# Holding back the first store and the fifth load until four loads have landed, in a gate-and-dispatch kernel

## The chip, the cores and the metric

The kernel runs on one core of a Trainium2 chip. The metric is the device time in microseconds (us) of one execution. Every profile below is one profiled execution; its "span" goes from the first to the last instruction of the program and is about 2 us shorter than the device time.

## The reference

For each of 16 x 1024 = 16384 tokens, the router has 8 logits. The two largest probabilities are taken and scaled to add up to one; each token's row of 512 numbers is then written twice, once for each of the two, multiplied by its weight.

```python
probs = softmax(router_logits)                       # over 8 experts
topk_probs = the two largest of probs, smaller first
topk_probs = topk_probs / sum(topk_probs)
out = x[:, :, None, :].repeat(2, axis=2) * topk_probs[..., None]
```

The input x has 33.6 MB, the logits 0.5 MB, the output 67.1 MB, all float32.

## The kernel before

Tokens are laid over 128 partitions, M = 128 tokens to a partition. `top2_weights` (lines 14 to 43) is done once for all tokens: one load of the logits (line 74), a small tournament of maxima and minima on VectorE that ends with the difference of the two largest logits (line 39), and two sigmoids on ScalarE (lines 41 and 42), which give the two weights `WA`.

The rest is one loop (line 77) over 16 chunks of L = 8 tokens per partition. Each chunk does three things:

- line 80: a load of 2 MB (2048 KB), issued by SyncE, from x into a tile `xg`. The pool `xbufs` has four buffers, so the first four loads are issued at once and each later load waits until the multiply four chunks earlier has freed its buffer.
- line 82: one multiply on VectorE, 128 x 8192, which reads `xg` twice through a broadcast and writes the tile `og`. The pool `obufs` has three buffers, so from the fourth chunk on a multiply waits until an earlier store has landed.
- line 88: a store of 4 MB (4096 KB), issued by ScalarE, from `og` to the output.

The loads stand in SyncE's queue and the stores in ScalarE's, each in order: what stands behind a waiting issue waits as well. Both queues are served by the same 16 DMA engines; in the profile the loads are queue q1 and the stores queue q10. The semaphores, the buffer assignment and the order on each queue are made by a scheduler when the program is built. Chunks, loads, multiplies and stores are counted from 0 in numbers (load 3 is the fourth).

Of the kernel before, what the change touches and what calls it, by code (L numbers as in the profile page):

```python
# [1 line left out]

# [4 lines left out]

F32 = mybir.dt.float32
ALU = mybir.AluOpType
ACTF = mybir.ActivationFunctionType  # L10
P = 128


def top2_weights(nc, pool, logits, M, E):

    hi, lo, n = None, None, E
    while n > 1:  # L20
        n //= 2
        if hi is None:
            a, b = logits[:, :, 0:n], logits[:, :, n : 2 * n]
            nhi = pool.tile([P, M, n], F32, tag=f"hi{n}")
            nlo = pool.tile([P, M, n], F32, tag=f"lo{n}")
            nc.vector.tensor_tensor(nhi, a, b, op=ALU.max)  # L26
            nc.vector.tensor_tensor(nlo, a, b, op=ALU.min)  # L27
        else:
            a, b = hi[:, :, 0:n], hi[:, :, n : 2 * n]
            nhi = pool.tile([P, M, n], F32, tag=f"hi{n}")  # L30
            nlo = pool.tile([P, M, n], F32, tag=f"lo{n}")
            tmp = pool.tile([P, M, n], F32, tag=f"tmp{n}")
            nc.vector.tensor_tensor(tmp, lo[:, :, 0:n], lo[:, :, n : 2 * n], op=ALU.max)  # L33
            nc.vector.tensor_tensor(nlo, a, b, op=ALU.min)  # L34
            nc.vector.tensor_tensor(nlo, nlo, tmp, op=ALU.max)  # L35
            nc.vector.tensor_tensor(nhi, a, b, op=ALU.max)  # L36
        hi, lo = nhi, nlo
    dlt = pool.tile([P, M], F32, tag="dlt")
    nc.vector.tensor_tensor(dlt, hi[:, :, 0], lo[:, :, 0], op=ALU.subtract)  # L39
    WA = pool.tile([P, M, 2], F32, tag="WA")  # L40
    nc.scalar.activation(WA[:, :, 0], dlt, ACTF.Sigmoid, scale=-1.0)  # L41
    nc.scalar.activation(WA[:, :, 1], dlt, ACTF.Sigmoid, scale=1.0)  # L42
    return WA


@with_exitstack
def kernel(
    ctx: ExitStack,
    tc: tile.TileContext,
    x: bass.AP,  # L50
    router_logits: bass.AP,
    k: bass.AP,
    out: bass.AP,
):
    nc = tc.nc
    B, S, D = x.shape
    E = router_logits.shape[-1]
    N = B * S
    assert int(k) == 2 and E == 8 and N % P == 0
    M = N // P  # L60

    L = 8
    x_v = x.rearrange("b s d -> (b s) d").rearrange("(p m) d -> p m d", p=P)
    o_v = out.rearrange("b s k d -> (b s) k d").rearrange("(p m) k d -> p m k d", p=P)
    rl_v = router_logits.rearrange("b s e -> (b s) e").rearrange(
        "(p m) e -> p m e", p=P
    )

    wpool = ctx.enter_context(tc.tile_pool(name="wpool", bufs=1))
    xbufs = ctx.enter_context(tc.tile_pool(name="xbufs", bufs=4))  # L70
    obufs = ctx.enter_context(tc.tile_pool(name="obufs", bufs=3))

    logits = wpool.tile([P, M, E], F32)
    nc.sync.dma_start(logits, rl_v)  # L74
    WA = top2_weights(nc, wpool, logits, M, E)

    for c in range(M // L):
        rows = slice(c * L, (c + 1) * L)
        xg = xbufs.tile([P, L, D], F32, tag="xg")
        nc.sync.dma_start(xg, x_v[:, rows, :])  # L80
        og = obufs.tile([P, L, 2, D], F32, tag="og")
        nc.vector.tensor_tensor(  # L82
            og,
            xg.unsqueeze(2).to_broadcast([P, L, 2, D]),
            WA[:, rows, :].unsqueeze(3).to_broadcast([P, L, 2, D]),
            op=ALU.mult,
        )
        nc.scalar.dma_start(o_v[:, rows], og)


# [1 line left out]
_INS = ['x', 'router_logits', 'k']  # L92
_OUTS = [((16, 1024, 2, 512), 'float32')]

_NUMBERS = {'k': 2}


# [26 lines left out]
```

## Time and profile before

| what | value |
|---|---|
| device time, median of 3 (lowest to highest) | 246.81 us (245.37 to 248.87) |
| span of the profiled execution | 244.8 us |
| VectorE busy, of which the 16 multiplies | 142.6 us, 138.9 us |
| one multiply (line 82) | 8.69 us |
| one load, 2048 KB: median from issue to landing | 42.3 us |
| one store, 4096 KB: median from issue to landing | 35.6 us |
| moved in all, mean rate over the span | 101.19 MB, 413 GB/s |

The page's digit rows cut the span into 40 slices of 6.1 us and give the busy share of each in tenths. "DMA" is the mean busy share of the 16 DMA engines, and "GB/s" is what they moved. The time from issue to landing holds the time in which a transfer stood behind others in its queue. The chain of waits goes back from the last instruction to what released it, and so on; "DMA out_dram<-og" is a store, "DMA xg<-in_x_dram" a load, "DVE og L82" a multiply. In tables of stretches each row names the stretch, its length, each engine's busy time with the number of instructions in it, the TensorE clock (unused here), the DMA engines' busy share and the rate.

### The profile page before, as it was taken

How to read it: one execution, taken by the hardware profiler on the slowest of the kernel's cores; microseconds unless marked ns; L12 is line 12 of the kernel's file. 1: busy time of each engine (PE TensorE's matmuls, PEld its weight loads, DVE VectorE, ACT ScalarE, POOL GpSimd, SP SyncE). 2: the span in 40 equal slices, each digit the busy share in tenths (PEclk: the TensorE clock that was granted, in tenths of full speed). 3: DMA queues.
4: the chain of work that ended last, by engine and by line, in shares of the span. 5: the costliest groups of instructions: out<-in, count | busy, mean ns of one | idle time of the engine just before them, and what ended most of it. 6: DMA issues, size and time to landing. Idle time of an engine off the chain costs nothing.

```text
span 244.8 us, 149 instructions
## 1 busy us (share of the span) xinstructions
DVE 142.6 (58%) x27; ACT 1.8 (1%) x3; POOL 0.2 (0%) x4
## 2 busy tenths in 40 slices
DVE  3799978549093580936729185391763908585000
ACT  2000000000000000000000000000000000000000
POOL 0000000000000000000000000000000000000000
DMA  7999999899999999999999999999999999999981
GB/s 300 428 428 332 439 428 471 385 436 452 428 439 412 428 458 420 396 428 431 442 439 420 426 447 407 452 404 399 466 423 415 426 418 434 428 428 428 434 369 86
DMA packets 4752, 101.19 MB, mean 413 GB/s; under 512 B 528, under 2 KB 528, under 8 KB 656
## 3 DMA queue, kind: packets, MB, share of 16 engines
q10 hardware_dynamic: 2304, 67.11, 63.9%
q1 hardware_dynamic: 2448, 34.08, 33.4%
HBM read 34.08 MB, written 67.11 MB: 413 GB/s over the span
## 4 chain that ended last, share of the span: by engine, by line
DMA 69%; DVE 21%; issue 0%; SPq 0%; DVEq 0%
DMA out_dram<-og 66%; DVE og L82 21%; DMA xg<-in_x_dram 3%; SPq L74 0%; DVEq L82 0%
## 5 line engine op out<-in xcount | busy, mean ns | idle before, releaser
L82 DVE TENSOR_TENSOR og<-xg,WA 128x8192 f32<-128x8192 f32 x16 | 138.9, 8691 | 77.2 <-DMA out_dram<-og 75.9
L26 DVE TENSOR_TENSOR nhi<-logits 128x512 f32<-128x512 f32 x1 | 0.7, 693 | 3.9 <-DMA logits<-in_router_logits_dram 3.9
L41 ACT ACT_TABLE_LOAD x1 | 1.3, 1283 | 0.7 <-PEq L105 0.7
L34 DVE TENSOR_TENSOR nlo<-nhi 128x256 f32<-128x256 f32 (+1 forms) x2 | 0.7, 353 | 0.0
L36 DVE TENSOR_TENSOR nhi<-nhi 128x256 f32<-128x256 f32 (+1 forms) x2 | 0.7, 353 | 0.0
L33 DVE TENSOR_TENSOR tmp<-nlo 128x256 f32<-128x256 f32 (+1 forms) x2 | 0.7, 352 | 0.0
L35 DVE TENSOR_TENSOR nlo<-nlo,tmp 128x256 f32<-128x256 f32 (+1 forms) x2 | 0.7, 352 | 0.0
L27 DVE TENSOR_TENSOR nlo<-logits 128x512 f32<-128x512 f32 x1 | 0.7, 683 | 0.0
L41 ACT ACTIVATE WA<-dlt 128x128 f32<-128x128 f32 x1 | 0.3, 315 | 5.7 <-DVE dlt L39 5.7
L39 DVE TENSOR_TENSOR dlt<-nhi,nlo 128x128 f32<-128x128 f32 x1 | 0.3, 291 | 0.0
L42 ACT ACTIVATE WA<-dlt 128x128 f32<-128x128 f32 x1 | 0.3, 299 | 0.0
L105 POOL MEMSET const-bfloat16-1.0<- 128x1 bf16 x1 | 0.1, 103 | 0.0
L105 POOL MEMSET const-uint8-127<- 128x1 uint8 x1 | 0.1, 102 | 0.0
L105 POOL MEMSET const-float32-0.0<- 128x1 f32 x1 | 0.1, 100 | 0.2 <-issue 0.2
L105 POOL MEMSET const-float32-1.0<- 128x1 f32 x1 | 0.1, 99 | 0.0
## 6 DMA issues: line engine op xcount, KB each, us to landing
out_dram<-og ACTq DMA_DIRECT2D x16, 4096.0 KB, 35.6
xg<-in_x_dram SPq DMA_DIRECT2D x16, 2048.0 KB, 42.3
logits<-in_router_logits_dram SPq DMA_DIRECT2D x1, 512.0 KB, 3.1
```

Source lines behind the costliest of these rows:

```text
L26: nc.vector.tensor_tensor(nhi, a, b, op=ALU.max)
L27: nc.vector.tensor_tensor(nlo, a, b, op=ALU.min)
L33: nc.vector.tensor_tensor(tmp, lo[:, :, 0:n], lo[:, :, n : 2 * n], op=ALU.max)
L34: nc.vector.tensor_tensor(nlo, a, b, op=ALU.min)
L35: nc.vector.tensor_tensor(nlo, nlo, tmp, op=ALU.max)
L36: nc.vector.tensor_tensor(nhi, a, b, op=ALU.max)
L39: nc.vector.tensor_tensor(dlt, hi[:, :, 0], lo[:, :, 0], op=ALU.subtract)
L41: nc.scalar.activation(WA[:, :, 0], dlt, ACTF.Sigmoid, scale=-1.0)
L42: nc.scalar.activation(WA[:, :, 1], dlt, ACTF.Sigmoid, scale=1.0)
L82: nc.vector.tensor_tensor(og, xg.unsqueeze(2).to_broadcast([P, L, 2, D]), WA[:, rows, :].unsqueeze(3).to_broadcast([P, L, 2, D]), op=ALU.mult,
L105: nc = _bacc.Bacc("TRN2", target_bir_lowering=False, num_devices=1)
```

## The change

Two dependencies are added by hand, both on the landing of load 3 (the fourth, `AHEAD - 1`): load 4 is not issued before load 3 has landed, and neither is the store of chunk 0. The purpose is to have the first four input buffers filled before any output traffic takes part of the DMA engines.

```diff
+    AHEAD = 4
+    sync = mybir.DependencyInfo(
+        mybir.DependencyClass.Sync, mybir.DependencyReason.DATA
+    )
+    gate = None
     for c in range(M // L):
         rows = slice(c * L, (c + 1) * L)
         xg = xbufs.tile([P, L, D], F32, tag="xg")
-        nc.sync.dma_start(xg, x_v[:, rows, :])
+        load = nc.sync.dma_start(xg, x_v[:, rows, :])
+        if c == AHEAD - 1:
+            gate = load.ins.name
         og = obufs.tile([P, L, 2, D], F32, tag="og")
...
+        if c == AHEAD:
+            tc.add_manual_dep(load.ins, gate, sync, reason="join")
-        nc.scalar.dma_start(o_v[:, rows], og)
+        store = nc.scalar.dma_start(o_v[:, rows], og)
+        if c == 0:
+            first = store
+        if c == AHEAD - 1:
+            tc.add_manual_dep(first.ins, gate, sync, reason="join")
```

The instructions are the same in kind and number. In the program that the scheduler builds from this, the first stores on ScalarE's queue stand in another order than in the source (the tile numbers are those of the program: og_91 is chunk 0, og_96 chunk 1, og_101 chunk 2):

```
L97 out<-og_96    waits for VectorE (the multiply of chunk 1)
L97 out<-og_91    waits for the landing of load 3
L97 out<-og_101   waits for VectorE (the multiply of chunk 2)
```

The loads and the multiplies stand in the order of the source. The multiply of chunk 3 writes the buffer that chunk 1 used, and the multiply of chunk 4 the buffer of chunk 0.

## The prediction

> **What bounds the kernel now.** I began with the page's slices and queue totals, since a kernel that only multiplies and copies is likely bound by data movement.
>
> ```profile
> span 244.8 us, 149 instructions
> DVE 142.6 (58%) x27; ACT 1.8 (1%) x3; POOL 0.2 (0%) x4
> DMA  7999999899999999999999999999999999999981
> GB/s 300 428 428 332 439 428 471 385 436 452 428 439 412 428 458 420 396 428 431 442 439 420 426 447 407 452 404 399 466 423 415 426 418 434 428 428 428 434 369 86
> DMA packets 4752, 101.19 MB, mean 413 GB/s; under 512 B 528, under 2 KB 528, under 8 KB 656
> q10 hardware_dynamic: 2304, 67.11, 63.9%
> q1 hardware_dynamic: 2448, 34.08, 33.4%
> ```
>
> The reader is to see that the DMA digit is 8 or 9 from the second slice to the third-last: the two queues' packets fill 63.9% + 33.4% = 97.3% of the time of 16 engines. VectorE is busy only 58%. Next the waits (the second line is SyncE's queue):
>
> ```profile
> DVE og L82 <- DMA out_dram<-og: 75.9, 13, 7.1
> SPq L80 <- DVE og L82: 152.5, 12, 15.1
> ```
>
> Thirteen multiplies wait for a store to land, so that an output buffer comes free; twelve loads wait for a multiply to free an input buffer; after the first one no multiply waits for a load. This ring is driven by how fast stores land. The chain of waits in order of time gives the beginning of it:
>
> ```profile
> 1.15 7.74 DMA xg<-in_x_dram
> ...
> 8.99 8.70 DVE og L82
> 17.70 0.02 issue
> 17.72 19.83 DMA out_dram<-og
> 37.55 0.03 DVEq L82
> 37.58 0.04 issue
> 37.63 8.70 DVE og L82
> ```
>
> The first load lands at 8.9, the first multiply ends at 17.7, the first store leaves then and takes 19.8 us. Last, the stretches of time (length, VectorE, ScalarE and GpSimd busy, clock, DMA share, GB/s):
>
> ```profile
> 10.00:18.00 8.00, 8.00 (x2) 0.00 (x0) 0.00 (x0) 1.00 1.01 432
> 18.00:24.00 6.00, 6.00 (x1) 0.00 (x0) 0.00 (x0) 1.00 1.01 336
> 24.00:60.00 36.00, 27.24 (x4) 0.00 (x0) 0.00 (x0) 1.00 1.00 432
> 60.00:200.00 140.00, 79.26 (x10) 0.00 (x0) 0.00 (x0) 1.00 1.01 429
> 208.00:236.00 28.00, 12.40 (x2) 0.00 (x0) 0.00 (x0) 1.00 1.00 432
> 236.00:244.80 8.80, 0.00 (x0) 0.00 (x0) 0.00 (x0) 1.00 0.33 142
> ```
>
> This is the table on which the forecast rests. Loads alone (10 to 18) move at 432 GB/s, loads and stores mixed (24 to 60) at 432, stores alone (208 to 236) at 432. Keeping loads and stores apart therefore buys no rate. The span can be rebuilt: the first packet moves at 1.7 us, 101.19 MB / 432 GB/s = 234.2 us, and the losses are 0.3 us at the start (1.2 to 9 us ran at 387), 6 x (1 - 336/432) = 1.3 us when the first store starts, 140 x (1 - 429/432) = 1.0 us in the middle, and 8.8 x (1 - 0.33) = 5.9 us at the end, where a few of the 16 engines still work after the others are done. The sum is 1.7 + 234.2 + 0.3 + 1.3 + 1.0 + 5.9 = 244.4, against a span of 244.8. Bytes and these losses are all there is.
>
> **What the Trainium skill says.** "DMA: Bandwidth & Descriptors", section "Issuing engines are not separate DMA queues": transfers issued by different engines run on the same 16 DMA engines and interleave. The same page, "Queues, rings and completion order", has each engine take turns between its queues packet by packet. The trace agrees: stores (4.2 MB) and loads (2.1 MB) share 432 GB/s, and 6.29 MB / 432 = 14.6 us is the pace at which VectorE's later multiplies follow each other (14.5 to 15.8 us from the fourth to the fifteenth). The same page, "Anatomy of one DMA", gives about 2.0 us of fixed cost for a transfer, most of it the confirmation after the last byte. The logits load agrees: 3.1 us from issue to landing, of which 0.52 MB / 432 = 1.2 us is data, leaves 1.9 us.
>
> **The change part by part.** *The two dependencies in the program.* They add no instruction that moves data, so bytes, multiplies and buffers are as before. In the built program the scheduler has also put chunk 1's store ahead of chunk 0's on ScalarE's queue: the first store issued waits for the second multiply, and chunk 0's store, right behind it, for the fourth load. The fourth multiply takes chunk 1's output buffer, the fifth that of chunk 0, so buffers come free in the order of the stores.
>
> *The fifth load waits.* Loads 0 to 2 land at 8.9, 13.8 and 18.7 us (issues at 1.15, 1.6 and 2.1 plus 7.7, 12.2 and 16.6 to landing), so one load by itself takes 4.9 us. The fourth landed at 30.0 before (issued at 2.6, 27.4 to landing), since the first store and the fifth load joined it. With both held back it lands at 18.7 + 4.9 = 23.6. The fifth load, before issued at 17.7, is issued then. Queued behind it on SyncE is only the sixth load, which needs the second multiply's end at 26.3 anyway.
>
> *The hole in the DMA.* Up to 23.6 the engines have only the four loads, and the fifth is not handed over until the semaphore of the fourth has fired. So the engines run dry from the last byte of load 3 until the first byte of load 4: exactly the fixed part of one transfer, seen once. From below it is the time from issue to the first packet: the logits issue at 0.73 shows its first packet at 1.70, so 1.0 us. From above it is the 1.9 us of the logits plus the 0.3 us of the slow beginning, plus about 0.5 us for engines that finish early (in the landing records the engines of one early load lie 0.4 us apart): 2.7 us. I take 1.9, since the logits load contains both ends of it.
>
> *The first store waits.* Stores leave at 26.3 instead of 17.7, 8.6 us later. I price this at nothing, and the work that hides it is the loads: from about 24.7 load 4 has 4.9 us of bytes, and load 5 is issued at 26.3, so the engines have loads until store packets arrive. Stores moved back are loads moved forward. With the 19.8 us of the first store before, the first store lands near 26.3 + 19.8 = 46.1, and the fourth multiply starts there instead of at 37.6. Does either queue run dry after that? Load 7 can be issued when that multiply ends, near 54.9; loads 4, 5 and 6 are in the queue by 34.9, and at one load per 14.6 us they last to about 67. Three stores are in the queue by 34.9, and last to about 46.1 + 2 x 14.6 = 75; the next joins at 54.9. So both queues stay filled, by 12 us and more. At the end more stores run without loads beside them, at the same 432 GB/s, and with 9.7 us each (4.19 MB / 432) against 8.7 us for a multiply and three output buffers, VectorE keeps up.
>
> *The 1.3 us loss when the first store starts* I leave in place at its new time, because a load is again under way when the first store and another load are issued together. The stragglers' 5.9 us stay too: nothing in the change touches the engines' balance after 60 us.
>
> **Sum.** Span 244.8 + 1.9 = 246.7; the times are 2.0 us above the span (246.8 against 244.8), so 246.8 + 1.9 = 248.7 us, 0.8% slower, which 2% does not tell from no change.
>
> **The rivals.** *The hole is hidden or pays for itself.* The three times before spread from 245.4 to 248.9. If the loss of 1.3 us at the first store comes from the crowd of issues at 17.7 and goes away, the net is 1.9 - 1.3 = 0.6, so 247.4. For it: the later stores show no such loss. Against: a first store with loads under way is what the changed kernel has too. Chance 0.20.
>
> *Faster.* The engines that finish late could be put out of step by the first mixing, and a common restart at 23.6 could keep them together. With the 5.9 us gone: 248.7 - 5.9 = 242.8; with the 1.3 us gone too: 241.5, which alone is beyond 2% (below 241.9). For it: the fourth load, the first to be mixed, is the first whose landing stretches far beyond its 4.9 us. Against: from 24 to 60 the mixed rate is the full 432, so the lag is made later, where the change does not reach. Chance 0.10 in all, 0.03 beyond 2%.
>
> *Slower: the stores are the real path.* The chain of waits is 66% stores, and if it could not be caught up, the 8.6 us of late start would stand: 246.8 + 8.6 = 255.4. For it: every multiply from the fourth on waits for a store. Against: a store takes 35.6 us in the median only because it shares the engines with loads; with loads ahead, later stores go faster (stores alone at 432, from 208 on). Chance 0.06.
>
> **How the numbers follow.** Forecast 248.7 with 0.64; its cost bounds of 1.0 to 2.7 us give 247.8 to 249.5, and the scatter of the times of before (about 1.7 us each way) carries it further. To hold 8 in 10 the range takes in 247.4 and part of the faster case: 244.8 to 251.0. Beyond 2% slower is above 251.7: the store path, and a little for a larger tail: 0.08. Beyond 2% faster: 0.03. Within: 0.89.
>
> **What would show it.** In the changed profile: the fourth load lands near 23.6; a dip of about 2 us in the DMA right after; first store issued near 26.3, fourth multiply near 46; loads ending earlier beside the stores and more stores alone at the end; 432 GB/s between; a tail of about 6 us. Wrong would be: a second gap in the DMA digits after 40 us, which means a queue ran dry; a mixed rate away from 432; or a tail far from 6 us, which would mean that the engines' imbalance depends on how mixing starts.

## The result, and the profile after

The changed kernel takes 257.76 us (median of 4 runs, 257.44 to 258.16); the kernel before takes 247.31 (4 runs, 245.37 to 248.87). The ratio is 1.043, with a 95% interval of 1.035 to 1.051: 10.5 us slower, where 1.9 us had been forecast and 251.0 us was the top of the range. Here and below a median is over all runs, while a ratio compares on each side the runs within 1.5% of its fastest, so the two can differ.

The page of the changed kernel, the slices and queue totals:

```profile
span 256.3 us, 149 instructions
DMA  7997999999999999999999999999999994999940
GB/s 284 442 417 289 317 445 407 458 412 453 404 440 414 437 424 445 404 447 407 427 435 437 419 424 432 407 437 424 427 345 445 435 430 205 430 465 414 409 179 20
q10 hardware_dynamic: 2304, 67.11, 61.3%
q1 hardware_dynamic: 2448, 34.08, 32.4%
```

Bytes and instructions are unchanged. One dip is the forecast one (the fourth slice, 19 to 26 us; the fifth holds the beginning of the first store). Two are new: the 34th slice (211 to 218 us) at 205 GB/s, and a last stretch of some 10 us in which almost nothing moves. The packets' own time hardly changed: 93.7% of 256.3 us is 240.2 us, against 97.3% of 244.8 = 238.2. So the time went mostly to engines that had nothing to do.

The waits of the changed kernel (the last two lines are SyncE's queue):

```profile
DVE og L89 <- DMA out_dram<-og: 86.9, 13, 12.3
SPq L85 <- DVE og L89: 157.3, 11, 20.7
SPq L85 <- DMA xg<-in_x_dram: 20.5, 1, 20.5
```

The new wait of load 4 is the last line, once, 20.5 us. Otherwise the ring is the old one, and thirteen multiplies still wait for a store, 11.0 us longer in total (86.9 against 75.9). From the changed kernel's chain of waits, in order of time:

```profile
9.39 17.30 DVE og L89 x2
26.69 0.02 issue
26.71 20.76 DMA out_dram<-og
47.48 0.03 issue
...
47.60 8.70 DVE og L89
...
56.32 38.25 DMA out_dram<-og
...
103.42 40.65 DMA out_dram<-og
...
152.87 39.86 DMA out_dram<-og
```

The first store leaves at 26.71 and lands at 47.5; then each step of the chain is a store of some 40 us and a multiply, so three stores, one ring turn of three output buffers, take about 49 us, or 16.5 us per chunk (103.42 to 152.87 is 49.45). The pace should be 14.6. The stretches of time (length, VectorE, ScalarE and GpSimd busy, clock, DMA share, GB/s):

```profile
10.00:22.00 12.00, 12.00 (x2) 0.00 (x0) 0.00 (x0) 1.00 1.01 434
22.00:26.00 4.00, 4.00 (x1) 0.00 (x0) 0.00 (x0) 1.00 0.46 152
26.00:40.00 14.00, 9.28 (x2) 0.00 (x0) 0.00 (x0) 1.00 1.01 386
40.00:60.00 20.00, 8.69 (x1) 0.00 (x0) 0.00 (x0) 1.00 1.00 432
60.00:100.00 40.00, 22.69 (x3) 0.00 (x0) 0.00 (x0) 1.00 1.00 428
100.00:180.00 80.00, 41.09 (x6) 0.00 (x0) 0.00 (x0) 1.00 1.01 427
180.00:200.00 20.00, 12.95 (x2) 0.00 (x0) 0.00 (x0) 1.00 0.98 402
200.00:210.00 10.00, 4.13 (x2) 0.00 (x0) 0.00 (x0) 1.00 1.02 441
210.00:220.00 10.00, 9.20 (x2) 0.00 (x0) 0.00 (x0) 1.00 0.69 295
220.00:247.00 27.00, 14.24 (x2) 0.00 (x0) 0.00 (x0) 1.00 0.95 410
247.00:256.00 9.00, 0.00 (x0) 0.00 (x0) 0.00 (x0) 1.00 0.05 22
```

Rebuilt as in the prediction, with length x (1 - rate/432) for each stretch: 1.7 before the first packet, 0.4 up to 22 us (1.2 to 10 ran at 385), 234.2 of bytes, 2.6 (22 to 26) and 1.5 (26 to 40) at the hole and the first store, 0.4 + 0.9 in the middle, 1.4 (180 to 200), -0.2 (200 to 210), 3.2 (210 to 220), 1.4 (220 to 247) and 8.8 from 247 on. The sum is 256.3, which is the span. The hole and the first store cost 4.1 us, where the prediction had 1.9 + 1.3 = 3.2. All after 60 us costs 15.9, where it had 1.0 + 5.9 = 6.9. Nine of the missing 9.6 us lie there, long after both new waits are over.

Yet the mean DMA share from 60 to 180 is full. What the share hides is shown by the landing records: every transfer is split over 16 DMA engines, and the trace has a landing for each. For stores of the changed kernel, counted in the order in which they leave (store 0 is chunk 1's, store 1 is chunk 0's), in us from the span's start:

```
store    median engine   15th of 16    last     last - median
  1          61.70          61.98      62.01         0.3
  4         105.42         105.66     111.12         5.7
  7         146.62         149.40     160.32        13.7
  9         173.68         178.38     192.72        19.0
 15         246.56         246.66     255.45         8.9
```

One engine falls behind, from 1.4 us at store 2 to 19.0 at store 9, or 2.5 us per store. The Trainium skill, "DMA: Bandwidth & Descriptors", section "Why a DMA increments its semaphore by 16 and not by 1", says that the 16 engines of a transfer finish independently and that only the full count means that the data has landed. The trace agrees: the multiply that reuses the buffer starts at 111.2, 160.4 and 192.8, some 0.1 us after the last landing and up to 19 us after the median one. So the ring turns at the pace of the slowest engine, the other 15 run dry (180 to 200, 210 to 220), and the late one works on alone for the last 9 us. In the kernel before, five engines were late together, by 4 to 6 us at the end.

The packet records show where the lag comes from. Put in chains, each packet where another one ends, they show that an engine takes one load packet (16 KB, 0.611 us) and one store packet (32 KB, 1.213 us) in turn, as the skill's section "Queues, rings and completion order" of the same page says. The page puts a packet at 9 to 17 descriptors as a rule; here each packet is one row of a tile. Eight packets and one completion record of 4 bytes make up an engine's share of a transfer, and the completion takes a turn as well, which the page does not say: on the late engine a store packet runs from 108.902 to 110.548 us, and only then does the completion of load 9 start, at 110.551, and that of store 4 at 110.560. From about 65 us on, many store packets of this engine last 1.4 to 1.7 us instead of 1.213, which makes up some 1.0 to 1.6 us per 10 us; the load packets keep their 0.611. Why they stretch is not in the records.

### The profile page after: what moved, and what is told of

Its sections match the earlier page's. It is cut to its first block, busy times and chain, and to the rows that moved or that the text cites. A ratio compares the mean times of both kernels' runs of the same rounds, so it can differ in the third digit from the quotient of the medians.

```text
span 256.3 us, 149 instructions
## 1 busy us (share of the span) xinstructions
DVE 142.6 (56%) x27; ACT 1.8 (1%) x3; POOL 0.2 (0%) x4
## 4 chain that ended last, share of the span: by engine, by line
DMA 67%; DVE 24%; issue 0%; SPq 0%; DVEq 0%
DMA out_dram<-og 64%; DVE og L89 24%; DMA xg<-in_x_dram 3%; SPq L74 0%; DVEq L89 0%
## 5 line engine op out<-in xcount | busy, mean ns | idle before, releaser
L89 DVE TENSOR_TENSOR og<-xg,WA 128x8192 f32<-128x8192 f32 x16 | 138.9, 8691 | 88.1 <-DMA out_dram<-og 86.9
```

The costliest lines, as they stand in the source:

```text
L89: nc.vector.tensor_tensor(og, xg.unsqueeze(2).to_broadcast([P, L, 2, D]), WA[:, rows, :].unsqueeze(3).to_broadcast([P, L, 2, D]), op=ALU.mult,
```

## The experiments

The experiments are about why one engine's store packets stretch. The expectations name theory S: what counts is where the loads' packets fall against the stores' packets in the turns of an engine. In the kernel before a load ends, on the median engine, 5.5 us after a store; in the changed kernel load 6 and store 1 end at 61.80 and 61.70, and load 7 and store 2 at 76.40 and 76.27, that is, together ("in step"). The rivals are defined where they stand. A means used throughout is a tiny extra load into a spare tile that nothing reads: it shifts all later loads by its packets and its completion, so by a known number of turns on each engine, and moves at most 0.13 MB (0.3 us at 432 GB/s). The kernel before, run beside the experiments, had medians of 246.2 to 247.5 us. Where runs of one kernel lie far apart, all of them or their spread are given, since a median alone would mislead.

**The two halves of the change.** Only the load waits:

```diff
-        store = nc.scalar.dma_start(o_v[:, rows], og)
-        if c == 0:
-            first = store
-        if c == AHEAD - 1:
-            tc.add_manual_dep(first.ins, gate, sync, reason="join")
+        nc.scalar.dma_start(o_v[:, rows], og)
```

> Only the fifth load waits for the fourth; the stores are as in the kernel before. Theory S (step): in the changed kernel load c+5 and store c of each DMA engine run in step (their last packets fall together), and in that state one engine's store packets are stretched, which costs the 10 us. Here the first store leaves at 17.7 and load 4 starts near 30.5, so loads end about two packets before the stores: not in step, 247 to 249 us. Theory D (depth): the loads are so far ahead that few are in the queue, and the ring follows the slowest engine. Here the loads are behind, so the queue is deep: 247 to 249. Theory O (order and hole): the two swapped stores and the gap in the DMA do it; both are absent: 247. All three expect no loss; a loss would put it on the load's wait alone.

Measured: 248.94 us (247.77 to 250.20, 20 runs), ratio 1.009 (1.007 to 1.012). Loads end 1.3 to 2.0 us ahead of stores on the median engine, no engine is alone at the end, and several lag, by up to 8.4 us. The late wait of a load by itself costs about 2 us, not 10. Only the first store waits:

```diff
-        if c == AHEAD:
-            tc.add_manual_dep(load.ins, gate, sync, reason="join")
```

> Only the first store waits (and the scheduler again puts chunk 1's store ahead of chunk 0's); the fifth load leaves at 17.7 as before. S: load 4 runs on without a hole, so when the first store's packets come (about 30 us) load 5 is some three packets in; loads end three packets before the stores, not in step: 246 to 249 us. D: the loads are even further ahead and their queue even emptier: 255 to 259. O: the order is swapped, there is no hole: about 257 if the order does it, 247 if the hole does.

Measured: a median of 248.47 us, but from 241.14 to 258.05 in 20 runs, six of them above 254. I had expected this geometry to put the loads three packets ahead; in fact load 6 and store 1 end together (58.73 and 58.90). In the profiled run (250.51 us) six engines are late together, by 8 to 9 us at the end. No single answer comes from it, except that the store's wait alone can bring the loss and that what follows from it differs from run to run.

**Out of step, into step.** The changed kernel with a tiny load after load 6, of 64 partitions (four packets and a completion per engine, five turns) or of 16 (two turns):

```diff
+        if c == 6:
+            pad = spare.tile([P, 256], F32, tag="pad")
+            extra = nc.sync.dma_start(pad[0:64, :], x_v[0:64, 0, 0:256])
+            tc.add_manual_dep(extra.ins, third.ins.name, sync, reason="join")
```

Here `third` is the multiply of chunk 2, for which load 6 waits anyway; the shorter one reads `pad[0:16, :]` from `x_v[0:16, 0, 0:256]`.

> The changed kernel with one tiny extra load (64 partitions of 1 KB, four packets on each DMA engine, into a buffer that nobody reads) in the loads' queue between load 6 and load 7. It costs no bandwidth, but in the turns between the two queues it puts the loads four packets behind the stores from about 61 us on. S: the step is broken before the slow engine appears (65 us): 248 to 250 us. D: depth and order as in the changed kernel: 257 to 258. O: 257 to 258.

> As the changed kernel with the tiny load between load 6 and load 7, but with one packet on each DMA engine (16 partitions) instead of four. S, if only exact step is harmful: 249 to 252 as with four packets. If closeness to the step matters gradually: between, 252 to 256. D: 257 to 258.

Measured: 251.21 us (249.24 to 252.76, 4 runs), ratio 1.014 (1.006 to 1.023), for five turns, and 249.23 (244.79 to 251.61, 20 runs), ratio 1.003 (0.999 to 1.007), for two. Both hold both waits of the change and the hole. Five turns is about 1 us above what S had said, but the lone late engine is gone in both, although the two stores are still swapped and the hole is there, so neither of these (rival O) makes the loss by itself. The page with two turns:

```profile
span 248.3 us, 149 instructions
DMA  6996999999999999999999999999999999999991
GB/s 274 435 430 296 327 406 417 459 409 437 442 422 428 451 420 443 430 412 420 425 454 401 425 404 425 446 412 409 404 441 414 438 428 422 428 433 449 433 396 58
```

The forecast dip at the fourth slice is there, the gap at 211 us is not, and the end is short. A tiny load of 16 KB takes off some 8 us. As controls, the same tiny load with 128 partitions is a whole transfer of nine turns, which puts the place back: in the changed kernel (`pad[0:128, :]`, after load 6), and in the kernel before (after load 4, with no wait added):

```diff
+        if c == 4:
+            pad = spare.tile([P, 256], F32, tag="pad")
+            nc.sync.dma_start(pad[0:128, :], x_v[0:128, 0, 0:256])
```

> Control for the tiny load in the changed kernel: with eight packets on each engine (128 partitions) instead of one or four, plus its completion, it takes a whole transfer's turns, so loads again end with stores. If the place of loads against stores counts: 254 to 259, as the changed kernel, perhaps with a run far below. If any tiny load cures: 249 to 251.

> Control for the five-packet load in the kernel before: the same tiny load with eight packets on each engine (128 partitions), a whole transfer's number of turns, so that loads again end three packets after stores, one store later. S: as the kernel before, 245 to 249. If the tiny load itself did the harm: 254 to 258.

Measured: 257.44 us (257.13 to 258.54, 4 runs), ratio 1.047 (1.038 to 1.056), in the changed kernel, and 247.20 (244.94 to 249.33, 20 runs), ratio 1.004 (1.001 to 1.007), in the kernel before. So the tiny load by itself neither heals nor harms by more than 0.7%; what counts is by how many turns it shifts the loads. Then the kernel before was put into step, with 80 partitions (six turns) and 64 partitions (five, one short of step on the median engine):

```diff
+            nc.sync.dma_start(pad[0:80, :], x_v[0:80, 0, 0:256])
```

> The kernel before with one tiny extra load (80 partitions of 1 KB, five packets on each DMA engine, into a buffer that nobody reads) between load 4 and load 5. Before, each load ends three packets after a store; five more make eight, a whole transfer, so that loads and stores run in step. Nothing waits that did not wait before. S: a slow engine appears, 253 to 259 us. D: the loads' queue is deeper than before, 247. O: no swap, no hole: 247.

> The kernel before with a tiny load of four packets on each engine, one turn short of the five that brought the step. If only the step itself is harmful: 245 to 250. If nearness is enough: 252 to 258.

Measured with six turns: 258.30, 257.73, 258.13 and 243.65 us. With five: a median of 256.72 over 20 runs, sixteen of them above 254 and four between 245.25 and 249.47. The page of six turns:

```profile
span 256.5 us, 150 instructions
DMA  7999999999999999999999999999999999693941
GB/s 286 422 437 365 442 432 430 426 429 422 434 414 434 432 422 419 416 427 429 416 416 419 424 422 429 422 422 411 447 406 424 457 414 416 281 409 158 409 210 61
```

No hole after four loads, no wait, no reordered store, and yet the late gaps of the changed kernel (281 and 158 GB/s) and its loss. In the profiled runs of both kernels three engines are late, by 9 to 15 us at store 9. This shows that the loss needs neither of the change's waits. With five turns it was open whether one turn short is enough: mostly it is. But the place on the median engine does not decide alone: the kernel in which only the load waits has its loads in the same place there (1.3 to 2.0 us ahead of the stores, here 1.6 to 1.9), and none of its 20 runs was above 250.20.

**Rivals: depth, addresses, chance.** Does the loss hang on how deep the loads' queue is (D)? With five input buffers instead of four:

```diff
-    xbufs = ctx.enter_context(tc.tile_pool(name="xbufs", bufs=4))
+    xbufs = ctx.enter_context(tc.tile_pool(name="xbufs", bufs=5))
```

> The changed kernel with five input buffers instead of four: every load can leave one chunk earlier, so the loads' queue holds one transfer more all along, and the order of packets, and with it the step, stays. S: 255 to 258 as before. D (the shallow queue lets one engine hold up the ring): 248 to 251.

Measured: 245.59, 254.56, 257.89 and 260.35 us; in the profiled run (260.35) one engine is 15.3 us late at store 9, and all others are within 1.2 us of the median. Depth does not remove it from three of four runs. Does it hang on which addresses are read while which are written? In this kernel every load reads chunk 0's rows, so that what it leaves out is the other fifteen chunks of x, and its output is chunk 0's rows with every chunk's weights:

```diff
-        load = nc.sync.dma_start(xg, x_v[:, rows, :])
+        load = nc.sync.dma_start(xg, x_v[:, 0:L, :])
```

> The changed kernel with every load reading the rows of chunk 0, so that what is read from the memory hardly moves (the output is then that of chunk 0's rows, weighted). Turns, sizes and waits are as before. If the stretched packets come from reads and writes that hit the same part of the memory as both walk through it, the slow engine goes or moves: 245 to 252. If they come from the turns of the two queues alone: 256 to 258.

Measured: 257.45, 258.12, 258.72 and 253.02 us, with the one slow engine. The walk of the read addresses is not needed for the loss; the addresses of the stores were not varied. And the changed kernel as it is, once more:

> The changed kernel as it is, beside the others on the same chip, to see whether its time is always near 258 or spreads, as the two other kernels that turned out to run in step did (loads ending within 1 us of stores: 241 to 258 us with only the store held back, 244 to 258 with the five-packet load). S: mostly 255 to 258, possibly a run far below when no engine turns slow. D and O: always 257 to 258.

Measured: 256.96 us (256.81 to 257.44, 4 runs), ratio 1.041 (1.035 to 1.048). Store 9 lands at 191.64 with its last engine and at about 174.5 with the median one.

**In step on all engines.** Stores 0 and 1 both wait for load 3, so that stores go out in the order of the source:

```diff
-        if c == 0:
-            first = store
+        if c < 2:
+            early.append(store)
         if c == AHEAD - 1:
-            tc.add_manual_dep(first.ins, gate, sync, reason="join")
+            for one in early:
+                tc.add_manual_dep(one.ins, gate, sync, reason="join")
```

> The changed kernel with the stores of chunks 0 and 1 both held back for the fourth load, which keeps them in the order of the source; the first store then leaves near 24 instead of 26.7. O (the swap does it): 248 to 250. S: the order is of no account, what counts is where the loads then fall; if a load's end lies within some 1.2 us of a store's end, 255 to 258, else 248 to 251.

Measured: 250.22 us (249.70 to 251.40, 4 runs), ratio 1.026 (1.014 to 1.037). S had expected 255 to 258 and missed. Loads end 0.2 us before stores, but on all 16 engines. The stretches of this kernel:

```profile
60.00:180.00 120.00, 66.84 (x9) 0.00 (x0) 0.00 (x0) 1.00 1.01 412
180.00:200.00 20.00, 13.77 (x2) 0.00 (x0) 0.00 (x0) 1.00 1.00 426
200.00:240.00 40.00, 20.82 (x3) 0.00 (x0) 0.00 (x0) 1.00 0.99 425
240.00:248.00 8.00, 0.00 (x0) 0.00 (x0) 0.00 (x0) 1.00 0.85 365
```

The packets of all engines are stretched (412 GB/s at a full share; 0.4 to 0.6 us per 10 us each), and so no engine waits for another: the end is sharp, 0.85 instead of 0.05. Being in step is thus not enough for the large loss. In the profiled runs above 255 us of kernels with two queues one to three engines are late at the end; with six (250.51 us) and with all in step (250.58) the loss is small. The same kernel with the tiny load of five turns after load 6:

> The changed kernel with stores 0 and 1 both held back (250.2 us), plus the tiny load with four packets on each engine between load 6 and load 7. If the loss shared by all engines belongs to the step: 246.5 to 249, and stretched packets on few engines. If it belongs to the start of the mixing: 250.

Measured: 251.96 us (250.24 to 253.71, 4 runs), ratio 1.024 (1.015 to 1.033), and not the 246.5 to 249 expected. The common stretching went, but five engines lag instead, by 6 to 9 us at the end.

**A sharper sign, and a test of it.** With these traces side by side I compared, for stores 4 to 10 of each profiled run, the last landing of the store with the nearest last landing of a load:

| profiled run | last store after last load, us | last minus median engine at store 10, us | median time of the kernel, us |
|---|---|---|---|
| before | -7.4 to -6.3 | 4.8 | 246.2 to 247.5 |
| before, nine turns | -7.3 to -5.7 | 4.2 | 247.20 |
| only the load waits | 2.4 to 3.1 | 7.6 | 248.94 |
| changed, two turns | -5.5 to -4.7 | 3.7 | 249.23 |
| changed, five turns | 4.6 to 5.2 | 6.6 | 251.21 |
| in order, five turns | -7.5 to -7.3 | 8.1 | 251.96 |
| **changed** | **0.20 to 0.21** | **18.9** | **257.76** |
| **changed, again** | **0.18 to 0.19** | **18.3** | **256.96** |
| **changed, nine turns** | **0.17 to 0.18** | **13.3** | **257.44** |
| **changed, five buffers** | **0.18 to 0.19** | **16.6** | **256.23** |
| **changed, same rows** | **0.16** | **18.7** | **257.78** |
| **before, six turns** | **0.16 to 0.19** | **16.8** | **257.93** |
| **before, five turns** | **0.18** | **15.7** | **256.72** |
| only the first store waits | 0.17 to 0.21 | 10.8 | 248.47 (241 to 258) |
| both stores wait, in order | 0.15 to 0.18, on all engines | 0.4 | 250.22 |

Every slow kernel (in bold) has the same 0.2 us, transfer after transfer, on its late engine. Of the others, the last two have it as well, and the rest come no nearer than 2.4. I call it the lock: on that engine the completion of a load directly precedes that of a store. A landing carries no engine's number; that the two last landings belong to one engine is taken from the constant distance and from the completion records that stand next to each other (110.551 and 110.560 above). The table also bears on five turns in the kernel before: the median engine ends its loads 1.8 us before its stores, but the late engine is locked. The kernels without the lock lag too, though less (3.7 to 8.1 us at store 10). To see whether the lock causes the loss while it lasts (S) or the start decides all (B), I broke it in the middle: the tiny load comes after load 10, with two turns and with five.

```diff
-        if c == 6:
+        if c == 10:
             pad = spare.tile([P, 256], F32, tag="pad")
...
-        if c == 2:
+        if c == 6:
             third = mul
```

> The changed kernel, with a tiny extra load of 16 partitions by 1 KB (two turns of the loads' queue) between load 10 and load 11, that is, in the middle of the run and not before it has gone wrong. Theory S in its sharper form, the lock: in every slow trace so far the last engine's load lands 0.16 to 0.21 us before the last engine's store, transfer after transfer, and in no trace without the loss (there it is 2.4 us or more). While an engine is in that place its store packets are stretched. S expects: until about 125 us as the changed kernel (the last engine of store 5 or 6 some 8 to 11 us behind the median); from load 11 on the distance leaves 0.2 us, the lag stops growing at some 10 to 14 us instead of 19, and since about half of the stretching is saved, the time is 251 to 254. Rival B (what is lost is fixed by how the run begins, and the place of the two queues later on does not matter): the lag grows on to 19 us, and the time is 256 to 258.

> As the kernel with the late break of two turns, but the tiny load has 64 partitions (five turns). S expects the same: distance away from 0.2 us from load 11 on, 251 to 254. B expects 256 to 258. If only one of the two breaks the lock, the size of the shift decides where the late engine ends up, since it lies some 11 us behind the others at that time and so in another place of the turns than they do.

Measured: 255.30 us (252.95 to 255.98, 4 runs), ratio 1.042 (1.031 to 1.052), with two turns; 254.19 (251.55 to 256.51, 4 runs), ratio 1.035 (1.022 to 1.048), with five. Landings of the profiled run with two turns:

```
store   last     last - median   nearest load, last store after last load
  4    111.22         5.7         load  9    0.18
  5    127.12         7.9         load 10    0.18
  6    142.69        10.1         load 11   -1.87
  7    158.03        11.5         load 12   -1.84
  8    172.92        12.3         load 13   -1.86
  9    188.13        13.6         load 14   -1.84
```

Up to load 10 it is the changed kernel, with 2.1 us of lag per store; from load 11 on the lock is broken, and the lag grows by 1.2 per store ((13.6 - 10.1) / 3), little more than half as fast. The pace of the last engine is the clearer sign. After the break its stores come 15.1 us apart (142.69 to 188.13, three times), against 16.2 in the changed kernel between stores 6 and 9 (144.06 to 192.72). The seven kernels in bold have 16.1 to 16.6 there, the six at the head of the table 15.2 to 15.9, and the break with five turns 15.0. With five turns the growth falls from 1.5 us per store (1.1 at store 3, 4.0 at store 5) to 0.4 (5.5 at store 6, 6.6 at store 9). The page of two turns:

```profile
span 253.5 us, 150 instructions
GB/s 279 424 427 305 313 414 447 416 452 411 458 424 429 409 440 416 421 434 414 442 437 421 414 414 458 421 424 424 442 409 440 421 437 346 471 372 414 476 134 21
```

The gap at 211 us has shrunk from 205 GB/s to 346 and 372. Both medians lie below B's 256 to 258, by 0.7 and 1.8 us, and above S's range, by 1.3 and 0.2. The times by themselves hardly separate S from B: the changed kernel was not run beside these two, and the kernel before took 246.21 us there, about 1 us less than beside the other experiments. The landings do: the lock slows its engine while it lasts, and lag made before the break is not recovered.

**A kernel without two queues.** If turn-taking is the trouble, all transfers on SyncE's queue should escape it:

```diff
-        nc.scalar.dma_start(o_v[:, rows], og)
+        nc.sync.dma_start(o_v[:, rows], og)
```

> The kernel before with the stores issued by SyncE, on the same queue as the loads, so that the packets of loads and stores no longer take turns: each engine works off whole transfers in order (the scheduler groups them by threes). If stretched store packets arise only where the two queues take turns, there are none here, all engines end together, and the 5.9 us tail of before and the 1.0 us in the middle go: 247.1 - 5.9 - 1.0 = 240 us, up to 244 with small gaps where a group of stores waits for its multiply. If the stretching belongs to an engine or to stores as such, the tail stays: 246 to 250.

Measured: 262.42 us (261.89 to 262.52, 4 runs), ratio 1.063 (1.055 to 1.071). The program then has loads and stores in groups of three. From its waits and its page:

```profile
DVE og L82 <- DMA xg<-in_x_dram: 102.1, 6, 20.3
```

```profile
DMA  6999999998999989999999999999999999995077
GB/s 271 435 420 402 402 483 402 339 432 354 483 402 402 483 307 430 390 402 483 402 402 369 412 420 407 402 483 402 339 410 435 420 407 402 483 327 236 0 322 322
```

The engines do end together (within 0.2 us), as expected, but multiplies now wait for loads behind stores, each of the five changes from stores to loads shows a dip (slices of 307 to 369 GB/s), and the last chunk goes through load, multiply and store alone. At these changes packets do stretch: near 95 and 142 us load packets last over 0.8 us instead of 0.611, so the premise of the next expectation, that no packet was stretched here, does not hold. The same queue with loads and stores one by one, four loads ahead (`load` is a function that takes a buffer and starts one):

```diff
+    tiles = [load(c) for c in range(4)]
+    for c in range(C):
...
+        nc.sync.dma_start(o_v[:, rows], og)
+        if c + 4 < C:
+            tiles.append(load(c + 4))
```

> Loads and stores on SyncE's one queue again, but written so that the order is loads 0 to 3, then store 0, load 4, store 1, load 5 and so on, so that no group waits for a multiply. In the run with one queue in groups no packet was stretched and all engines ended within 0.2 us of each other; its loss was in the gaps. If taking turns between two queues is what stretches packets, this has neither: 1.7 + 234.2 + about 3 of starting and ending losses, 240 to 243 us, faster than both kernels by over 2%. If gaps come back where the one queue waits: 246 or more.

Measured: 251.85 us (250.02 to 253.11, 6 runs), ratio 1.031 (1.022 to 1.041), not the 240 to 243 expected. Its page:

```profile
GB/s 269 431 429 376 418 345 408 418 314 434 387 361 439 356 418 405 384 429 395 431 421 447 421 405 455 392 455 413 439 413 429 439 410 437 439 429 439 418 439 157
q1 hardware_dynamic: 4752, 101.19, 98.1%
```

The queue is filled (98.1%), the rate is not: up to 107 us slices in which loads follow stores fall to 314 to 387, and it is the load packets that stretch (one in twenty lasts 1.1 us or more). Stretched packets thus do not need two queues. Giving up the two queues costs more than it brings, and no version here beats the kernel before by its median; single runs of the first store's wait alone (241.14 and 241.46) are faster than every run of the kernel before beside them (the fastest took 244.53).

## Why the prediction was wrong

*What bounds it.* Right. The kernel stays bound by the ring of stores; no multiply after the first ones waits for a load. But 14.6 us was taken for the pace of the multiplies, which is their shortest step. From the fourth to the fifteenth of the kernel before

```profile
37.63 8.69 DVE L82 TENSOR_TENSOR og<-xg,WA 128x8192 f32<-128x8192 f32 x1 [2.74 <-DMA out_dram<-og]
...
203.01 8.69 DVE L82 TENSOR_TENSOR og<-xg,WA 128x8192 f32<-128x8192 f32 x1 [6.55 <-DMA out_dram<-og]
```

the mean is (203.01 - 37.63) / 11 = 15.0. The 0.4 us more per chunk is engines falling behind: the last landing is 0.2 us behind the median one at store 0 and 6.0 at store 12. So the ring followed its slowest engine already before, which its DMA share of 1.01 from 60 to 200 us does not show.

*The fifth load waits.* Right: load 3 landed at 23.96 (forecast 23.6) and load 4 was issued at 24.06.

*The hole.* Right in place and roughly in size: 22 to 26 us loses 2.6 us, of which a part belongs to the first store's beginning. Hole and first store together are 4.1 us instead of 3.2.

*The first store waits, at no price.* Its times were right (issued 26.71 against 26.3; fourth multiply 47.6 against 46; load 7 issued 56.3 against 54.9), and the lateness as such is cheap: the changed kernel with two turns keeps it and takes 249.23, within 0.6 us of the forecast 248.7. But the new start times also set where loads and stores end against each other, and that was not asked.

*"The stragglers' 5.9 us stay too: nothing in the change touches the engines' balance after 60 us."* This is the step that failed. The engines' balance after 60 us depends on where the start puts loads against stores. The term was 1.0 + 5.9 = 6.9 us and measured 15.9. The runs showed in its place a late engine whose loads end 0.2 us before its stores, whose store packets are stretched while this lasts, and for which the multiplies wait. Two or five turns of shift take it away, nine leave it, and six or five turns bring it into most runs of the kernel before, without any wait.

*The rivals.* "Faster" had the right idea, that the start sets the engines' balance, with the wrong sign: in the changed kernel the restart does not keep them together. Where both stores wait it does (0.4 us at store 10), and the price is 412 GB/s from 60 to 180 us, where the kernel before moves 428. "Slower: the stores are the real path" gave 255.4, near the measured time, by a mechanism that the runs deny: a first store 8.6 us late costs 8.6 us in none of the shifted kernels. It was not the answer with a small chance; its number was right by accident. "The hole is hidden" falls with the dip of 2.6 us.

*What would show it.* The prediction had written that a tail far from 6 us would mean that the engines' imbalance depends on how mixing starts. The tail is 8.8 us, so this sign came true. The gap at 211 us was foreseen only as a queue that runs dry; engines did run dry there, but because the output buffers came free only when the late engine landed.

*What stays open.* Why a store packet is stretched in this place at all, why the lock, once there, holds from transfer to transfer, which and how many engines fall into it, why the kernel in which only the load waits never does, and why the first store's wait alone gives anything from 241 to 258 us. Single runs of kernels whose profiles have the lock were fast (243.65, 245.59); they were not profiled, so whether they had it is not known. That the place of loads against stores causes the loss is shown by shifting it in and out with a control. That the lock on the late engine is how it does so is supported by its break in mid-run, but six engines can have it at a small loss; its physical cause is not known.

## What to carry to other kernels

When two queues keep the DMA engines full, a mean share near 1 says nothing on balance: compare the last of the 16 landings of a transfer with the median one, store by store, and suspect one or a few late engines when the difference grows. In this kernel a wait at the start changed for the whole run where the two queues' transfers end against each other. Such an effect has to be priced as well, and before the loss is given to the wait itself it is worth trying a tiny extra transfer of a few packets, with one of a whole transfer's turns as a control.

## What the runs showed of the hardware that was not expected

- On one engine the two queues alternate strictly, load packet (0.611 us) and store packet (1.213 us), and a transfer's completion takes a turn too (in the changed kernel load 9's comes at 110.551 us, after a store packet that ends at 110.548), so a transfer of eight packets has nine turns; an extra load of 16 KB, two turns, made the changed kernel 8 us faster.
- In the changed kernel many store packets of 32 KB stretch from 1.213 us to between 1.4 and 1.7 on an engine whose loads end 0.2 us before its stores. With all 16 engines in that place the stretching is shared (0.4 to 0.6 us per 10 us) and costs little: 250.22 us.
- In one queue, a change from stores to loads showed as a dip to between 307 and 387 GB/s in a slice of 6 us, while two queues mixed packet by packet moved 428 to 432 in the kernel before.
